# A hybrid gated-attention and Hyena block on one core: the order of high and low products, the opening, the copies out of PSUM and the two layer norms are changed

## The chip, the cores and the metric

The kernel runs on one core of one Trainium2 chip. The metric is device time in microseconds (us) of one execution. Before the change it is 1891.8 us, the median of three runs (1891.52 to 1891.81).

## The reference, cut to what matters

The input is `x`, 256 tokens of 2048 channels, float32. One block is computed:

- One projection `x @ w_in` gives q, k (1024 channels each), v, r (2048 each), two gate vectors of rank 16, `u` (3 x 2048) and `g` (2 x 2048).
- Branch 1 is bidirectional gated linear attention over four heads, with an RMS norm, a SiLU gate from r and an output projection (2048 x 2048).
- Branch 2 is an order-2 Hyena operator: a short convolution splits `u` in v, x1, x2; each of two long convolutions is done by Fourier transforms, with filters that a small sine network makes; then comes an output projection.
- The branches are merged by sigmoid gates and go through `w_out` (2048 x 2048). `z = ALPHA*x + mix`, then a layer norm: `(z - mean) * rsqrt(var + eps) * g + b`.
- An MLP of 2048 -> 8192 -> 2048 with squared ReLU, `z = ALPHA*h + mlp`, and a second layer norm give the output.

Each weight is used once for 256 tokens, and all is float32 in and out.

## The kernel before, in words

**Two-part numbers.** A float32 number is written as a high part (rounded to the type `float32r`, which TensorE multiplies in one pass) and a low part, the remainder. `split_hi_lo` (L80) makes both: ScalarE (ACT in the profile) casts the high part (L81), VectorE (DVE) subtracts to get the low part (L82). A product of two such numbers needs three terms: high*high, high*low, low*high.

**Weights.** All weights lie in `wblk`, in blocks of 128 x 2048 float32 (1 MB), in the order of use. `fetch` (L89) loads a block on SyncE's queue into a `raw` tile (three buffers) and splits it in two halves of 1024 columns (tags `whi` and `wlo`, three half buffers each). Blocks 0 and 1 are loaded in halves, and the transposed input `xT` is loaded in four pieces of 512 KB between the halves of block 0 (`load_x`, L210).

**Two kinds of product.** `channel_pair` (L133) makes outputs with channels on the partitions: two blocks, each one output tile of 128 channels x 256 tokens. For each of 16 k-tiles it issues a high weight product (L143) whose moving operand is the activation's high and low part side by side, 512 columns, and then a low weight product (L144) with the high part alone, 256 columns. Then ACT copies the second half of the PSUM tile (L146), DVE adds it to the first (L147), and `pump` runs side work that has come due (gates, attention scores, filters, transforms, all with times in units of blocks). `token_products` (L151) makes outputs with tokens on the partitions: the activation is the stationary operand, and three products of 512 columns follow each other (L162 to L164) for each token half. `column_products` (L778) does the same in two column halves of 256 (L790 to L792).

**Order.** The program is written in the order opening, gate vectors (`pa`, L367), q, k, r, v with attention, g1, the Hyena stages `u`, g2, `ho`, `w_out`, first norm, then ff1 and ff2 in four quarters, second norm. A scheduler then orders each engine's instructions by a time model; `tc.high_priority()` moves what is under it ahead of other ready work. Each engine runs its own list strictly in order.

**Opening** (L209 to L221): three warm-up products on a zero tile, then the loads above. The constants' loads (`filt_consts`, L237) are issued from ACT's queue.

**Inverse transform** (`hy_inv`, L650): six products of 256 columns for each of two token halves, for 16 pairs of channel group and order.

**First norm** (L813 to L834), per token half `tb`: last products, `add_mix` (L797) with statistics, `norm_scale` (L760), then six column chunks: ACT applies scale and shift (L774), DVE multiplies by the gain row (L775) and adds the bias row (L776). GpSimd (POOL) does the last two for the chunk 1536:2048. `turn` (L822) transposes a chunk on TensorE (L826) and splits it into `hT`. ff1's first output tile takes the first token half before the second (`by_tile`).

**Second norm** (L877 to L886): per token half, `column_products` of the last 512 columns, `add_ff` (L850), `norm_scale`, the same chunks, and a store of each chunk on SyncE's queue (L886).

Of the kernel before, what the change touches and what calls it, by code (L numbers as in the profile page):

```python
# [9 lines left out]
F32 = mybir.dt.float32  # L10
# [30 lines left out]
def block_kernel(  # L41
# [47 lines left out]
    def fetch(between=lambda n, h: None):  # L89
# [5 lines left out]
        if n > 1:  # L95
            nc.sync.dma_start(raw, wblk[n])
        parts = []
        for h in range(2):
            if n <= 1:
                hs = slice(h * D // 2, (h + 1) * D // 2)  # L100
                nc.sync.dma_start(raw[:, hs], wblk[n][:, hs])
                between(n, h)
            hi = wp.tile([P, D // 2], F32R, tag="whi", bufs=3, name=f"whi{n}_{h}")
            lo = wp.tile([P, D // 2], F32R, tag="wlo", bufs=3, name=f"wlo{n}_{h}")
            split_hi_lo(hi, lo, raw[:, h * 1024:(h + 1) * 1024])
            parts.append((hi, lo))
        queue.append(parts)

# [24 lines left out]
    def channel_pair(act, name, dst=None, scale=1.0, by_tile=False):  # L133
        if dst is None:
            dst = base.tile([P, 2, L], F32, tag="sum", name=f"{name}_s")
        for c in range(2):
            ps = psum_main(f"{name}_{c}").rearrange("p (a b) -> p a b", a=2)
            parts = next_block()
            for ts in ((slice(0, P), slice(P, L)) if by_tile and c == 0 else (slice(0, L),)):
                for kt in range(KT):  # L140
                    hi, lo = parts[kt // 8]
                    js = slice(kt % 8 * P, (kt % 8 + 1) * P)
                    MM(ps[:, :, ts], hi[:, js], act[:, kt, :, ts], start=(kt == 0), stop=False)  # L143
                    MM(ps[:, 0, ts], lo[:, js], act[:, kt, 0, ts], start=False, stop=(kt == KT - 1))  # L144
            low = base.tile([P, L], F32, tag="low", name=f"{name}_l{c}")
            nc.scalar.activation(low, ps[:, 1], AF.Copy, scale=scale)  # L146
            nc.vector.scalar_tensor_tensor(dst[:, c], ps[:, 0], scale, low, op0=ALU.mult, op1=ALU.add)  # L147
            pump()
        return dst
# [58 lines left out]

    with tc.tile_pool(name="xp", bufs=1) as xp:  # L209
        def load_x(n, h):  # L210
            for g in (2 * h, 2 * h + 1):
                xr = xp.tile([P, 4, L], F32, tag=f"xr{g}", name=f"xr{g}")
                nc.sync.dma_start(xr, xt[:, 4 * g:4 * g + 4, :])
                split_hi_lo(xT[:, 4 * g:4 * g + 4, 0], xT[:, 4 * g:4 * g + 4, 1], xr)

        wu = xp.tile([P, 512], F32, tag="wu", name="wu")
        nc.vector.memset(wu, 0.0)
        pw = psum_side("warm")
        for _ in range(3):
            MM(pw, wu[:, 0:P], wu, start=True, stop=True)  # L220
        fetch(load_x)  # L221
# [15 lines left out]
    def filt_consts():  # L237
        raw = fp.tile([P, 4, P], F32, tag="w4", name="dftraw")
        nc.scalar.dma_start(raw, dft_in)
        split_hi_lo(dfth, dftl, raw)  # L240
        mw = fp.tile([P, 3, P], F32, tag="mlpw", name="mlpw")
        nc.scalar.dma_start(mw, mlp_w)
        mc = fp.tile([P, 4], F32, tag="mlpc", name="mlpc")
        nc.scalar.dma_start(mc, mlp_c)
        et = fp.tile([P, L], F32, tag="emb", name="emb_sb")
        nc.scalar.dma_start(et, emb)
        nc.scalar.dma_start(ba_sb, ba)
        nc.scalar.dma_start(conv_sb, convp)
        nc.scalar.dma_start(mask_sb, mask_in)
        nc.scalar.dma_start(sgn_sb, sgn_in)  # L250
        nc.scalar.dma_start(ident, ident_in)
        fst["mw"], fst["mc"], fst["g"] = mw, mc, et
# [113 lines left out]

    pa = psum_main("pa").rearrange("p (a b) -> p a b", a=2)  # L367
    fetch()
    parts = next_block()
    for kt in range(KT):  # L370
        hi, lo = parts[kt // 8]
        js = slice(kt % 8 * P, (kt % 8 + 1) * P)
        MM(pa, hi[:, js], xT[:, kt], start=(kt == 0), stop=False)
        MM(pa[:, 0], lo[:, js], xT[:, kt, 0], start=False, stop=(kt == KT - 1))
# [7 lines left out]
    k_sb = qp.tile([P, 8, L], F32, tag="k", name="k_sb")  # L382
    for dst, nm, sc in ((q_sb, "q", 1.0 / 16.0), (k_sb, "k", 1.0)):
        for c2 in range(4):
            channel_pair(xT, f"{nm}{c2}", dst[:, 2 * c2:2 * c2 + 2, :], sc)
# [162 lines left out]
    for h in range(HEADS):  # L548
        later(0, gla_gates(h))
        later(3, gla_scores(h))  # L550
        vh = gp.tile([P, NT, 512], F32R, tag="vh", name=f"vh{h}")
        vl = gp.tile([P, NT, 512], F32R, tag="vl", name=f"vl{h}")
        pss = token_group(xT, f"v{h}")
        for tb in range(NT):
            split_hi_lo(vh[:, tb], vl[:, tb], pss[tb])
        v_sb[h] = (vh, vl)
        later(1, gla_out(h))
# [92 lines left out]
    def hy_inv(c, o):  # L650
        def run():
            yh, yl = cst.pop(("Y", c, o))
            py = psum_side(f"yp{c}{o}")
            for tb in range(NT):
# [114 lines left out]
    CHUNKS = ((0, 256), (256, 256), (1536, 512), (512, 512), (1024, 256), (1280, 256))  # L769

    def norm_chunk(z, rows, tb, at, n, rs, nb):
        zc = z[:, tb, at:at + n]
        eng = nc.gpsimd if at == 1536 else nc.vector
        nc.scalar.activation(zc, zc, AF.Identity, scale=rs, bias=nb)  # L774
        eng.tensor_tensor(zc, zc, rows[:, 0, at:at + n], op=ALU.mult)  # L775
        eng.tensor_tensor(zc, zc, rows[:, 1, at:at + n], op=ALU.add)  # L776
# [36 lines left out]
    for tb in range(NT):  # L813
# [16 lines left out]
        for at, n in CHUNKS:  # L830
            norm_chunk(z1, rows1, tb, at, n, rs, nb)
            if at < 1536:
                turn(at, n)
        turn(1536, 512)  # L834
# [4 lines left out]
    def ff1(qi):  # L839
        f = act_tile(ep, "f", f"f{qi}") if qi % 2 == 0 else act_tile(base, "xT", f"f{qi}")  # L840
        for c2 in range(8):
            r = channel_pair(hT, f"f{qi}_{c2}", by_tile=(qi == 0 and c2 == 0))
# [7 lines left out]
    def add_ff(ps, tb, at, n, qi):  # L850
# [26 lines left out]
    pss = [[psum_main(f"w2_33_{tb}{ch}") for ch in range(2)] for tb in range(NT)]  # L877
    for tb in range(NT):
        column_products(pss, fts[3], parts, [tb], 0)
        with tc.high_priority():  # L880
            for ch in range(2):
                add_ff(pss[tb][ch][:, 0:256], tb, 1536 + ch * 256, 256, 3)
            rs, nb = norm_scale(st2, tb, "2")
        for at, n in CHUNKS:
            norm_chunk(z1, rows2, tb, at, n, rs, nb)
            nc.sync.dma_start(out[tb * P:(tb + 1) * P, at:at + n], z1[:, tb, at:at + n])  # L886
# [127 lines left out]
```

## Time and profile before

| | us |
|---|---|
| median of three runs | 1891.8 |
| the profiled execution | 1891.83 |
| its span in the profile | 1890.0 |
| TensorE (PE) busy | 1860.4 (98%) |
| TensorE weight loads (PEld) busy | 1599.7 (85%) |
| DVE busy | 1313.6 (70%) |
| ACT busy | 949.5 (50%) |
| POOL busy | 38.3 (2%) |
| mean granted TensorE clock | 0.994 |
| traffic with HBM | 198 GB/s |

The profile is one execution. A matmul's recorded duration is longer than the step from its start to the next one's start, because matmuls overlap in the array: L143 shows 394 ns and L144 279 ns, and the two together start every 0.35 us. So TensorE's cost is read from starts, in the timeline, and not from durations. "[3.89 <-DVE xT L82]" behind a row says that the engine was idle for 3.89 us before it, until that DVE instruction ended.

### The profile page before, as it was taken

How to read it: one execution, taken by the hardware profiler on the slowest of the kernel's cores; microseconds unless marked ns; L12 is line 12 of the kernel's file. 1: busy time of each engine (PE TensorE's matmuls, PEld its weight loads, DVE VectorE, ACT ScalarE, POOL GpSimd, SP SyncE). 2: the span in 40 equal slices, each digit the busy share in tenths (PEclk: the TensorE clock that was granted, in tenths of full speed). 3: DMA queues.
4: the chain of work that ended last, by engine and by line, in shares of the span. 5: the costliest groups of instructions: out<-in, count | busy, mean ns of one | idle time of the engine just before them, and what ended most of it. 6: DMA issues, size and time to landing. Idle time of an engine off the chain costs nothing.

```text
span 1890.0 us, 25333 instructions
## 1 busy us (share of the span) xinstructions
PE 1860.4 (98%) x10060; PEld 1599.7 (85%) x10060; DVE 1313.6 (70%) x1702; ACT 949.5 (50%) x1286; POOL 38.3 (2%) x60
## 2 busy tenths in 40 slices
PE   8999999999999999999999998999999999999996
PEld 7887888888888888888888888888888888888886
DVE  6787968875789888888556567666555555555556
ACT  5555556674555555555544444444434443444343
POOL 0000000000000000000000001000000000000001
PEclk9999999999999999999999999999999999999998
DMA  7667764445555555565655764555555555545552
GB/s 289 231 225 251 265 228 161 140 142 204 195 195 199 199 194 189 197 223 191 212 197 183 285 216 153 188 193 186 196 186 198 180 199 187 192 180 199 191 189 110
DMA packets 60583, 375.09 MB, mean 198 GB/s; under 512 B 7216, under 2 KB 10928, under 8 KB 20912
## 3 DMA queue, kind: packets, MB, share of 16 engines
q1 hardware_dynamic: 46512, 324.03, 47.4%
q0 software_dynamic: 5888, 29.36, 4.2%
q10 hardware_dynamic: 8064, 20.07, 3.0%
q8 instruction: 79, 1.29, 0.3%
q14 instruction: 40, 0.33, 0.0%
HBM read 356.66 MB, written 16.78 MB: 198 GB/s over the span
## 4 chain that ended last, share of the span: by engine, by line
PE 93%; DVE 4%; ACT 1%; DMA 1%; issue 1%; ACTq 0%; DVEq 0%; SPq 0%
PE f L143 13%; PE f L144 6%; PE g L143 6%; PE w L163 6%; PE w L164 6%; PE w L162 6%; PE go L143 3%; PE ux L143 3%; PE uz L143 3%; PE uv L143 3%; PE g L144 3%; PE ho L143 3%; PE ho L144 2%; PE uv L144 2%; PE ux L144 2%; PE go L144 2%
## 5 line engine op out<-in xcount | busy, mean ns | idle before, releaser
L82 DVE TENSOR_TENSOR wlo<-raw,whi 128x1024 fp32r<-128x1024 f32 x596 | 728.3, 1223 | 488.2 <-ACT whi L81 487.3
L81 ACT CAST whi<-raw 128x1024 fp32r<-128x1024 f32 x596 | 627.0, 1053 | 772.6 <-PE w L164 186.8
L143 PE MATMUL f<-hT,whi 128*128 128x512 f32 (+1 forms) x1040 | 361.7, 394 | 0.0
L144 PE MATMUL f<-hT,wlo 128*128 128x256 f32 (+1 forms) x1040 | 290.0, 279 | 0.0
L143 PEld LDWEIGHTS f<-hT,whi 128*128 128x128 f32 x1040 | 195.6, 188 | 44.3
L144 PEld LDWEIGHTS f<-hT,wlo 128*128 128x128 f32 x1040 | 197.1, 190 | 0.1
L163 PE MATMUL w<-wlo,f 128*128 128x512 f32 x480 | 186.8, 389 | 0.0
L164 PE MATMUL w<-whi,f 128*128 128x512 f32 x480 | 186.8, 389 | 0.0
L143 PE MATMUL g<-xT,whi 128*128 128x512 f32 x512 | 178.6, 393 | 0.0
L162 PE MATMUL w<-whi,f 128*128 128x512 f32 x480 | 168.0, 389 | 0.0
L144 PE MATMUL g<-xT,wlo 128*128 128x256 f32 x512 | 143.5, 281 | 0.0
L143 PEld LDWEIGHTS g<-xT,whi 128*128 128x128 f32 x512 | 95.7, 187 | 21.1
L162 PEld LDWEIGHTS w<-whi,f 128*128 128x128 f32 x480 | 90.0, 188 | 18.8
L164 PEld LDWEIGHTS w<-whi,f 128*128 128x128 f32 x480 | 90.1, 188 | 18.7
L163 PEld LDWEIGHTS w<-wlo,f 128*128 128x128 f32 x480 | 90.1, 188 | 18.5
L144 PEld LDWEIGHTS g<-xT,wlo 128*128 128x128 f32 x512 | 96.7, 189 | 0.5 <-DVE wlo L82 0.2
L143 PE MATMUL uz<-xT,whi 128*128 128x512 f32 x256 | 91.9, 398 | 0.0
L143 PE MATMUL ux<-xT,whi 128*128 128x512 f32 x256 | 91.7, 398 | 0.0
L143 PE MATMUL go<-yg,whi 128*128 128x512 f32 x256 | 91.1, 397 | 0.0
L143 PE MATMUL uv<-xT,whi 128*128 128x512 f32 x256 | 90.5, 395 | 0.0
L143 PE MATMUL ho<-yh,whi 128*128 128x512 f32 x256 | 88.8, 391 | 0.0
L144 PE MATMUL ux<-xT,wlo 128*128 128x256 f32 x256 | 72.0, 281 | 0.0
(329 smaller groups left out, 3336.7 us busy)
## 6 DMA issues: line engine op xcount, KB each, us to landing
raw<-wblk SPq DMA_DIRECT2D x303, 1024.0 KB, 4.8
Td<-T POOLq DMA_DIRECT2D x16, 768.0 KB, 4.1
Tl<-Td POOLq DMA_DIRECT2D x16, 768.0 KB, 4.5
w<-w4s ACTq DMA_DIRECT2D x16, 512.0 KB, 4.6
zr<-ln_rows ACTq DMA_DIRECT2D x4, 1024.0 KB, 10.9
raw<-wblk SPq DMA_DIRECT2D x4, 512.0 KB, 6.7
xr<-xt SPq DMA_DIRECT2D x4, 512.0 KB, 6.5
dec<-decay_in ACTq DMA_DIRECT2D x8, 256.0 KB, 3.1
```

The source lines that it names most:

```text
L81: nc.scalar.copy(hi, src)
L82: nc.vector.tensor_tensor(lo, src, hi.bitcast(F32), op=ALU.subtract)
L143: MM(ps[:, :, ts], hi[:, js], act[:, kt, :, ts], start=(kt == 0), stop=False)
L144: MM(ps[:, 0, ts], lo[:, js], act[:, kt, 0, ts], start=False, stop=(kt == KT - 1))
L162: MM(pss[tb], sh, wh, start=(kt == 0), stop=False)
L163: MM(pss[tb], sh, wl, start=False, stop=False)
L164: MM(pss[tb], sl, wh, start=False, stop=(kt == KT - 1))
```

## The change

1. **Grouped products.** `channel_pair` issues, for each half of a block, eight high products and then eight low products.
2. **Opening by quarters.** Three blocks (`pa`, and the two of q's first pair) are opened together in three PSUM tiles. Weights and input are loaded in quarters (the first one, for block 0 and the input, in eighths), all issued first. Splits and products follow quarter by quarter.
3. **Constants** are loaded from POOL's queue and not from ACT's.
4. **Copies out of PSUM** of a channel block, and the split of v, stand under `tc.high_priority()`.
5. **`hy_inv`** makes six products of 512 columns, over both token halves.
6. **First norm**: five chunks, none of them on POOL; ff1's first two tiles take three of their four half blocks for the first token half, then for the second.
7. **Second norm**: the gain row is multiplied in when the columns are complete (`add_ff`). Token half 0 gets all 512 columns by `token_products`, and its norm is two DVE instructions per 512 columns (`affine`). For token half 1 TensorE makes `shift*gain + bias` in PSUM from plain float32 products (`ident` x bias row, `dg` x gain row, where `dg` is the identity times the shift), and DVE needs one instruction per chunk.

```diff
+    def channel_products(ps, act, half, kts, ts=FULL, opens=True):
+        hi, lo = half
+        at = [(kt, slice(kt % 8 * P, (kt % 8 + 1) * P)) for kt in kts]
+        for kt, js in at:
+            MM(ps[:, :, ts], hi[:, js], act[:, kt, :, ts], start=(kt == 0 and opens), stop=False)
+        for kt, js in at:
+            MM(ps[:, 0, ts], lo[:, js], act[:, kt, 0, ts], start=False, stop=(kt == KT - 1))
+
+    def channel_sum(dst, ps, name, scale=1.0):
+        low = base.tile([P, L], F32, tag="low", name=name)
+        with tc.high_priority():
+            nc.scalar.activation(low, ps[:, 1], AF.Copy, scale=scale)
+            nc.vector.scalar_tensor_tensor(dst, ps[:, 0], scale, low, op0=ALU.mult, op1=ALU.add)
 ...
+            for h in range(2):
+                channel_products(ps, act, parts[h], range(8 * h, 8 * h + 8))
+            channel_sum(dst[:, c], ps, f"{name}_l{c}", scale)
+            pump()
 ...
+    def channel_pair_by_tokens(act, name):
+        ps = [channel_psum(f"{name}_{c}") for c in range(2)]
+        blocks = [next_block() for _ in range(2)]
+        for ts in (slice(0, P), slice(P, L)):
+            for c, h in ((0, 0), (0, 1), (1, 0)):
+                channel_products(ps[c], act, blocks[c][h], range(8 * h, 8 * h + 8), ts,
+                                 opens=(c == 0 or ts.start == 0))
+        channel_products(ps[1], act, blocks[1][1], range(8, KT))
 ...
-        fetch(load_x)
+        for g in range(4):
+            n = 2 if g == 0 else 1
+            for i in range(n):
+                load_w(0, g, i, n)
+                load_x(g, i, n)
+            for b in range(1, OPENING):
+                load_w(b, g, 0, 1)
+        for g in range(4):
+            pieces = 2 if g == 0 else 1
+            for b in range(OPENING):
 ...
+                for i in range(n):
+                    split_hi_lo(hi[:, at:at + w], lo[:, at:at + w], raws[b][:, cs])
+                    if b == 0:
+                        split_hi_lo(xT[:, ks, 0], xT[:, ks, 1], xr[g][:, step * i:step * (i + 1)])
+                channel_products(open_ps[b], xT, halves_of[b], range(4 * g, 4 * g + 4))
 ...
-        nc.scalar.dma_start(raw, dft_in)
+        nc.gpsimd.dma_start(raw, dft_in)
 ...
-            for tb in range(NT):
-                dst = py[:, tb * CW:(tb + 1) * CW]
-                mm3(dst, dfth[:, 2], dftl[:, 2], yh[:, tb, 0], yl[:, tb, 0], True, False)
-                mm3(dst, dfth[:, 3], dftl[:, 3], yh[:, tb, 1], yl[:, tb, 1], False, True)
+            mm3(py3, dfth[:, 2], dftl[:, 2], yh[:, :, 0], yl[:, :, 0], True, False)
+            mm3(py3, dfth[:, 3], dftl[:, 3], yh[:, :, 1], yl[:, :, 1], False, True)
 ...
-    CHUNKS = ((0, 256), (256, 256), (1536, 512), (512, 512), (1024, 256), (1280, 256))
+    CHUNKS = ((0, 256), (256, 256), (512, 512), (1024, 512), (1536, 512))
 ...
-        eng = nc.gpsimd if at == 1536 else nc.vector
+        nc.vector.tensor_tensor(zc, zc, rows[:, 0, at:at + n], op=ALU.mult)
+        nc.vector.tensor_tensor(zc, zc, rows[:, 1, at:at + n], op=ALU.add)
 ...
+            nc.vector.tensor_tensor(zc, zc, rows2[:, 0, at:at + n], op=ALU.mult)   # add_ff, last quarter
 ...
+    def affine(tb, at, n, rs, nb):
+        nc.vector.scalar_tensor_tensor(t, rows2[:, 0, at:at + n], nb, rows2[:, 1, at:at + n], op0=ALU.mult, op1=ALU.add)
+        nc.vector.scalar_tensor_tensor(zc, zc, rs, t, op0=ALU.mult, op1=ALU.add)
 ...
+    token_products([ps], fts[3], parts, [0], 0)
+    add_ff(ps, 0, 1536, 512, 3)
+    rs, nb = norm_scale(st2, 0, "2")
+    for at in range(0, D, 512):
+        affine(0, at, 512, rs, nb)
+        store(0, at, 512)
+    column_products([None, pss], fts[3], parts, [1], 0)
+    for at, n in BIASED:      # (256, 512), (768, 512), (1280, 512), (1792, 256)
+        po[at] = psum_side(f"lo{at}")[:, 0:n]
+        tc.keep_in_program_order(MM(po[at], ident, rows2[:, 1, at:at + n], start=True, stop=False))
+    for ch in range(2):
+        add_ff(pss[ch][:, 0:256], 1, 1536 + ch * 256, 256, 3)
+    rs, nb = norm_scale(st2, 1, "2")
+    nc.vector.tensor_scalar(dg, ident, nb, None, op0=ALU.mult)
+    affine(1, 0, 256, rs, nb)
+    for at, n in BIASED:
+        MM(po[at], dg, rows2[:, 0, at:at + n], start=False, stop=True)
+        nc.vector.scalar_tensor_tensor(zc, zc, rs, po[at], op0=ALU.mult, op1=ALU.add)
+        store(1, at, n)
```

More of the change, by code (lines that the diff above doesn't have):

```diff
@@ L87, in block_kernel, with fetch @@
     stop_at = [W_OUT_END - 3]
-    def fetch(between=lambda n, h: None):
+    def fetch():
         n = fetched[0]
@@ L107, in fetch, with weight_half @@
         queue.append(parts)
+    def weight_half(n, h):
+        return (wp.tile([P, D // 2], F32R, tag="whi", bufs=3, name=f"whi{n}_{h}"),
+                wp.tile([P, D // 2], F32R, tag="wlo", bufs=3, name=f"wlo{n}_{h}"))
     side = []
@@ L136, in channel_pair @@
         for c in range(2):
-            ps = psum_main(f"{name}_{c}").rearrange("p (a b) -> p a b", a=2)
+            ps = channel_psum(f"{name}_{c}")
             parts = next_block()
[L139 to L147, printed above, removed]
+            for h in range(2):
+                channel_products(ps, act, parts[h], range(8 * h, 8 * h + 8))
+            channel_sum(dst[:, c], ps, f"{name}_l{c}", scale)
+            pump()
+        return dst
+    def channel_pair_by_tokens(act, name):
+        dst = base.tile([P, 2, L], F32, tag="sum", name=f"{name}_s")
+        ps = [channel_psum(f"{name}_{c}") for c in range(2)]
[5 more added lines that the diff above has]
+        channel_products(ps[1], act, blocks[1][1], range(8, KT))
+        for c in range(2):
+            channel_sum(dst[:, c], ps[c], f"{name}_l{c}")
             pump()
@@ L364, in block_kernel @@
         later(n + 2, filt_freq(c, o))
[L367 to L374, printed above, removed]
+    pa = open_ps[0]
     nc.scalar.copy(a_low, pa[:, 1])
@@ L382, in block_kernel @@
     k_sb = qp.tile([P, 8, L], F32, tag="k", name="k_sb")
+    for c in range(2):
+        channel_sum(q_sb[:, c], open_ps[1 + c], f"q0_l{c}", 1.0 / 16.0)
+        pump()
+    for _ in range(2):
+        fetch()
     for dst, nm, sc in ((q_sb, "q", 1.0 / 16.0), (k_sb, "k", 1.0)):
-        for c2 in range(4):
+        for c2 in range(1 if nm == "q" else 0, 4):
             channel_pair(xT, f"{nm}{c2}", dst[:, 2 * c2:2 * c2 + 2, :], sc)
@@ L553, in block_kernel @@
         pss = token_group(xT, f"v{h}")
-        for tb in range(NT):
-            split_hi_lo(vh[:, tb], vl[:, tb], pss[tb])
+        with tc.high_priority():
+            for tb in range(NT):
+                split_hi_lo(vh[:, tb], vl[:, tb], pss[tb])
         v_sb[h] = (vh, vl)
```

86 lines of the change are left out of this document (47 added, 39 removed).

## The prediction

> **What bounds the kernel now.** I read the page first, then busy time by stage, then the timeline of TensorE (PE) where it is not busy.
>
> ```profile
> PE 1860.4 (98%) x10060; PEld 1599.7 (85%) x10060; DVE 1313.6 (70%) x1702; ACT 949.5 (50%) x1286; POOL 38.3 (2%) x60
> ...
> PE 93%; DVE 4%; ACT 1%; DMA 1%; issue 1%; ACTq 0%; DVEq 0%; SPq 0%
> ```
>
> PE is busy 98% of the span and is 93% of the chain that ended last. So time goes only if PE's products get cheaper or its holes close. By stage (columns: length, then busy time of PE, PEld, DVE, ACT, POOL with counts, granted clock, DMA share, GB/s):
>
> ```profile
> 430.00:900.00 470.00, 470.00 (x2750) 412.46 (x2749) 395.52 (x475) 254.29 (x359) 15.23 (x28) 1.00 0.55 198
> ...
> 1128.00:1180.00 52.00, 46.41 (x342) 43.70 (x341) 39.63 (x72) 25.73 (x42) 5.71 (x4) 0.93 0.46 174
> ...
> 1846.00:1890.00 44.00, 29.60 (x220) 28.19 (x219) 26.76 (x53) 13.99 (x22) 6.32 (x4) 0.88 0.25 91
> ```
>
> In the middle PE never stops; holes are in the opening, around the first norm and behind the last product. Durations come from this execution: span 1890.0, its own time 1891.83, which is the median (1891.8). So I subtract from 1891.8.
>
> **1. Grouped products: -7.8.** Weight loads of the high products (L143), counted in two stretches of 80 us that hold nothing else (PE's second figure is the loads):
>
> ```profile
> 1230.00:1310.00 80.00, 80.00 (x232) 43.14 (x231) 1.00 0.54 196
> 1435.00:1515.00 80.00, 80.00 (x227) 42.48 (x227) 1.00 0.53 190
> ```
>
> 80/231 = 0.346 us for one high and one low product, 80/227 = 0.352: the same pair runs at two paces. Two streams of one size have one pace each: ff2's 512-column products start every 0.227 us (1547.48, 1547.71, 1547.94 in the timeline), the last 256-column ones every 0.120 (1856.00, 1856.12, 1856.24). 0.227 + 0.120 = 0.347 is the faster pace, so the slower one pays for the change of size from high to low (0.236 from a high start to the low one, where the fast pace has 0.230). Summed over the starts of the some 2,900 pairs that nothing interrupts, the excess over 0.347 is 8.9 us, 3.4 of it between 1400 and 1700, the rest mostly in q to `go`. Grouping keeps one change in eight: 8.9 x 7/8 = 7.8. Ends: 0 (the pace hangs on something else) and 8.9. Nothing shorter than 0.347 is to be had, as both streams show. What is late next? In 430 to 1100 the low half of a weight block is split at least 1.2 us, mostly 3.4, before its first product; a low product's half now gets 8 x 0.227 = 1.8 us more. The cover is thin only in 100-200 and 250-400, where the lead falls to 0.1.
>
> **2. `hy_inv` at full width: -1.25.** 16 calls lose 12 starts of 0.120 and get 6 of 0.227: 16 x (1.44 - 1.36) = 1.25. Ends 0.5 and 1.5. It lies in 500 to 900, all PE.
>
> **3. Opening: -5.0.**
>
> ```profile
> 3.36 3.02 PE L220 MATMUL warm<-wu 128*128 128x512 f32 x4
> 10.27 0.79 PE L373 MATMUL pa<-xT,whi 128*128 128x512 f32 x1 [3.89 <-DVE xT L82]
> ```
> ```profile
> 9.00:16.00 7.00, 5.73 (x18) 0.51 1.02 393
> ```
>
> PE idles until 10.27; then (second fence: PE's busy time, granted clock, DMA share, GB/s) the clock is halved until 15.9, so that pairs start every 0.64 us. The third block would end at 24.19 + 16 x 0.35 = 29.8 (a side product aside). The changed opening needs 5.24 MB for three blocks. Before has moved 1.2 MB by 7, 2.1 by 9, 3.2 by 12, 4.7 by 16 and 5.2 by 17 us. Taking these times, 0.7 us to landing, ACT casts of 0.6 (512 columns) and 1.05 (1024) and DVE differences of 0.69 and 1.23, the first products follow the warm-up at 6.4, wait once for the input's second eighth (0.8), and quarter 2 starts at 12.1; each quarter is 12 x 0.347 = 4.2 us of PE, so 16.4, 20.6, end 24.8. The fourth block's buffer is free at 18.3, its 1 MB lands at 22.8, cast by 23.9: in time. 29.8 - 24.8 = 5.0. Ends: 1 (the small pieces land as slowly as now, 6.7 us for 512 KB) and 6.5. The constants' loads on POOL's queue are hidden: `dftraw` can go at about 19, is cast behind the fourth block's first half at 24, and the transforms need it 50 us later; POOL's stores of 768 KB land in 4.1 us. If it came later than 25, ACT's next casts stand behind it, 1 us for 1 us.
>
> Here a rule speaks against the change. The Trainium skill (SBUF — State Buffer, on the engine and DMA doors) says that loads issued from POOL wait for descriptors while DVE runs an operation in its two-port mode. No row of before shows a load on POOL in the opening. If `dftraw`, whose issue falls among DVE's splits, waited for four of them at 1.2 us, it would land some 5 us later, and the sum would be 4 worse, which is the far end of the opening's range.
>
> **4. First norm: -2.5.**
>
> ```profile
> 1149.91 1.52 DVE L775 TENSOR_TENSOR zr<-zr 128x256 f32<-128x256 f32 x1
> ```
> ```profile
> 1162.52 0.99 PE L826 MATMUL ht<-ident,zr 128*128 128x128 f32 x4 [1.48 <-DVE zr L776]
> 1166.54 1.51 PE L826 MATMUL ht<-ident,zr 128*128 128x128 f32 x6 [3.03 <-DVE zr L776]
> ```
>
> That DVE product takes 1.52 us instead of 0.43 because POOL works on its chunk from 1149.86 to 1152.58; its neighbour L776 takes 1.51 likewise, and the same happens at 1163.03. Steps from start to start without POOL are 0.34 (256 columns) and 0.61 (512). Laying out DVE's list with these: token half 0 is done as early as now, half 1's shift comes at 1159.4 (now 1160.46), its columns up to 1536 at 1164.4, the last at 1165.7. PE has 24 half-width pairs of 0.23 for half 0 (5.5 us, now 3.7): busy to 1161.8, idle to 1164.9. Left then are 24 x 0.23 + 8 x 0.347 + 0.4 of transposes = 8.7, end 1173.6; now the two tiles end at 1178.6. At full clock that gains 5.0. But in before the clock was halved here (0.66 on average from 1160 to 1170) after idle spells of 1.5 and 3.0, so I expect it again, until about 1169.6: 4.7 us of work at half pace cost 2.3. I take 2.5; ends 1 and 5. The page TensorE: Matmul & The Clock Gate of the Trainium skill (Parts 1 and 4) says that a window of 3.4 us without activity halves the clock, and that transposes do not count as activity; by it the drop comes, and the sum is the one with 2.5.
>
> **5. Second norm: -2.1.**
>
> ```profile
> 1875.64 0.42 DVE L855 TENSOR_TENSOR zr<-zr,w 128x256 f32<-128x256 f32 x1 [1.69 <-PE w L792]
> ```
> ```profile
> 1880.88 2.76 DVE L775 TENSOR_TENSOR zr<-zr 128x512 f32<-128x512 f32 x2 [0.32 <-ACT zr L774]
> ...
> 1884.50 0.74 DVE L776 TENSOR_TENSOR zr<-zr 128x256 f32<-128x256 f32 x2
> ```
>
> Now: last addition 1875.64, shift known 1878.32, last DVE instruction 1885.24, end 1890.0 (store and landing, 4.75, which stays). After: half 0 costs 48 x 0.227 in place of 96 x 0.120, so PE ends 0.6 earlier, last addition at 1875.2 (DVE is still in `affine` of half 0: 8 x 0.61 from 1869). An `affine` instruction of 0.61 and the gain product of 0.34 stand ahead of the aggregate: shift at 1878.6, `dg` 0.2 later. Then TensorE needs 3.5 products of 512 plain float32 columns. The filter network's 256-column float32 products are two records that start 0.32 apart; for 512 I take 2 x 0.53 = 1.06 (ends 0.85, twice the warm-up's cold 0.85 record at full clock, and 1.7 at half clock): 1878.8 + 3.7 + 0.5 for the last DVE instruction and its wait = 1883.1. That gains 2.1; ends -0.3 (half clock) and 2.8. The bias products (3.7 us) lie beside the statistics and keep PE working until 1878.6.
>
> **6. Copies out of PSUM first: 0.** Each channel block has an ACT copy of 0.38 and a DVE sum of 0.42. Moved ahead, they push the next split back by as much, covered by the lead in 1. In q to attention (47 to 430, DVE busy 82%) PE waited 5.2 us in all, in single waits of 0.4 to 1.4 on `wlo`, `T` and `y`. These may go or double: -3 to +4.
>
> Sum: 7.8 + 1.25 + 5.0 + 2.5 + 2.1 = 18.65; 1891.8 - 18.65 = **1873.2**.
>
> **Rivals.**
> - *Grouping does nothing* (the slow pace belongs to the stage and not to the order): 1873.2 + 7.8 = 1881.0. For: the pace differs between equal stages (1230 and 1435). Against: ff2's stream beside it, at 1547, keeps 0.227. Chance 0.13.
> - *The clock holds at the first norm*, since half 0 now has 1.8 us more work: 1871. Against: the idle time is still 3 us. 0.15.
> - *The opening is held by transfers* or by the constants on POOL: gain 0 to 2, 1877. For: landing takes 6.5 us there. 0.10.
> - *The dense stages wait more*: four more waits of about 1 us in 47-430, 1877. 0.10. Or fewer waits and the better ends: 1867. 0.08.
> - *Slower*: the copies stand in ACT's and DVE's lists and wait for a block's last product, and the split behind them comes too late. Place: channel blocks with a lead under 0.8 us. There are some 90 between 47 and 900; were the lead gone in all of them at 0.4 us each, +36, so 1909; it decides from about 47 such blocks on (18.65/0.4). The lead of 1.2 to 3.4 speaks against it. 0.06.
>
> The forecast as summed gets 0.38. Cases within 1866 to 1882 hold over 0.8, so that is the range; the ends of parts 3 to 6 alone reach some 7 either way. A difference under 0.2% (3.8 us) can't be told from none here. Faster 0.92, same 0.02 (the dense stages' case with the worse ends of the others), slower 0.06.
>
> **What would show it.** Grouping: weight loads of the high products at 0.227, of the low ones at 0.120, in all stages. Opening: first real product at 6.4, third block done near 25. First norm: no DVE product of 256 columns above 0.45; two tiles done 5 us after half 1's transposes at full clock, 7 at half. Tail: 12.7 us from the last addition to the end (now 14.4), float32 products at 1.06. Wrong if PE shows holes between 430 and 1100, or pairs above 0.35.

## The result, and the profile after

The changed kernel takes 1883.31 us (median of five runs, 1880.54 to 1886.28) beside 1891.8 (five runs, 1891.52 to 1893.25): ratio 0.9951, 95% interval 0.9938 to 0.9963. It is faster, by 8.5 us and not by 18.6, and lies outside the range of the prediction. The profiled execution took 1880.54, the fastest of the five and 11.3 less than the profiled one before; the comparisons below are between these two. The two slowest of the five show a mean granted clock of 0.996 where the other three show 0.998 or 0.999, and 0.003 of 1880 us is 5.6 us, so by this estimate most of that spread goes with the lower clock.

First the page of the changed kernel: busy time, and the chain that ended last.

```profile
PE 1861.1 (99%) x9948; PEld 1597.5 (85%) x9948; DVE 1313.3 (70%) x1711; ACT 948.8 (51%) x1278; POOL 30.8 (2%) x61
...
PE 96%; DVE 2%; ACT 1%; DMA 0%; issue 0%; SPq 0%; DVEq 0%; ACTq 0%
```

PE has more of the chain (96%, was 93%), and its busy time has not fallen (1861.1, was 1860.4): 6.4 us of it are the new float32 products at the end (3.17 and 3.27), and the other products have not become as cheap as forecast. Busy time by stage (length, PE, PEld, DVE, ACT, POOL, granted clock, DMA share, GB/s; the last two stretches are moved with the stage):

```profile
430.00:900.00 470.00, 470.00 (x2671) 410.99 (x2671) 393.90 (x474) 257.96 (x360) 15.02 (x28) 1.00 0.54 200
1125.00:1177.00 52.00, 49.91 (x380) 47.45 (x379) 42.52 (x76) 27.18 (x42) 0.00 (x0) 1.00 0.52 198
1835.00:1878.60 43.60, 38.79 (x205) 31.50 (x203) 31.28 (x55) 9.67 (x13) 0.00 (x0) 0.99 0.31 120
```

The first norm has few holes left and a full clock (49.9 of 52, was 46.4 at 0.93), and so has the end (38.8 of 43.6, was 29.6 of 44 at 0.88).

Where the 11.3 us come from, by first products in the timeline of PE. "Waits" are steps over 60 ns longer than the stream's own, "pace" the rest above 0.227 or 0.120 us a start; what remains is products moved, added or saved.

| stretch | before | after | difference | of it waits, pace |
|---|---|---|---|---|
| first product to r | 127.6 | 124.9 | -2.7 | -2.6, -0.4 |
| r to v | 130.7 | 126.3 | -4.4 | -1.5, 0; 2.9 of products moved behind v |
| v to `uv` | 212.8 | 219.9 | **+7.1** | **+4.7**, -0.4; 2.7 of products moved in |
| `uv` to `ho` | 504.0 | 501.6 | -2.4 | -0.4, -0.7 |
| `ho`, w_out | 177.3 | 177.8 | +0.5 | 0, +0.6 |
| first norm, ff1's first quarters | 191.1 | 187.8 | -3.3 | -5.5, +1.1 |
| from ff2's first to the last main product | 530.3 | 527.5 | -2.8 | 0, -2.2 |
| last main product to end | 14.6 | 11.5 | -3.2 | |

Two things stand out. Pace has gained about 2 us in all. And g's first product is 8.6 us early (358.8, was 367.4), but `uv`'s first is at 472.6 in both. Not all of the 4.7 us lost there is idle time: right behind the hole shown below, the granted clock was 0.50 from 382.6 to 386.0, and 2.85 us of products ran in that window, which cost some 1.4 us (an estimate: half of 2.85).

### The profile page after: what moved, and what is told of

Same layout as the page of the kernel before. It is cut to its first block, busy times and chain, and to the rows that moved or that the text cites. A ratio compares the mean times of both kernels' runs of the same rounds, so it can differ in the third digit from the quotient of the medians.

```text
span 1878.7 us, 25104 instructions
## 1 busy us (share of the span) xinstructions
PE 1861.1 (99%) x9948; PEld 1597.5 (85%) x9948; DVE 1313.3 (70%) x1711; ACT 948.8 (51%) x1278; POOL 30.8 (2%) x61
## 4 chain that ended last, share of the span: by engine, by line
PE 96%; DVE 2%; ACT 1%; DMA 0%; issue 0%; SPq 0%; DVEq 0%; ACTq 0%
PE f L140 12%; PE f L142 6%; PE g L140 6%; PE w L188 6%; PE w L187 6%; PE w L189 6%; PE uv L140 3%; PE uz L140 3%; PE go L140 3%; PE ux L140 3%; PE ho L140 3%; PE g L142 3%; PE ho L142 2%; PE uv L142 2%; PE go L142 2%; PE ux L142 2%
## 5 line engine op out<-in xcount | busy, mean ns | idle before, releaser
L82 DVE TENSOR_TENSOR wlo<-raw,whi 128x1024 fp32r<-128x1024 f32 (+2 forms) x603 | 729.3, 1211 | 471.9 <-ACT whi L81 451.6
L81 ACT CAST whi<-raw 128x1024 fp32r<-128x1024 f32 (+2 forms) x603 | 627.4, 1041 | 770.7 <-PE w L189 188.8
L140 PE MATMUL f<-hT,whi 128*128 128x512 f32 (+1 forms) x1048 | 258.0, 388 | 0.0
L142 PEld LDWEIGHTS f<-hT,wlo 128*128 128x128 f32 x1048 | 142.3, 190 | 9.8
L142 PE MATMUL f<-hT,wlo 128*128 128x256 f32 (+1 forms) x1048 | 145.5, 282 | 0.0
L140 PE MATMUL g<-xT,whi 128*128 128x512 f32 x512 | 130.5, 396 | 3.7 <-DVE vl L82 3.7
L142 PEld LDWEIGHTS g<-xT,wlo 128*128 128x128 f32 x512 | 69.9, 190 | 5.0
L142 PE MATMUL g<-xT,wlo 128*128 128x256 f32 x512 | 71.8, 282 | 0.0
L140 PE MATMUL uz<-xT,whi 128*128 128x512 f32 x256 | 65.6, 394 | 0.0
L140 PEld LDWEIGHTS go<-yg,whi 128*128 128x128 f32 x256 | 46.1, 189 | 8.3
```

What stands on the lines that cost most here:

```text
L81: nc.scalar.copy(hi, src)
L82: nc.vector.tensor_tensor(lo, src, hi.bitcast(F32), op=ALU.subtract)
```

## The experiments

The three whose names begin with b are the kernel before or edits of it, all others edits of the changed kernel. Ratios are to the kernel before on the same chip, with 95% intervals; the changed kernel's is 0.9951.

### Pace: b0_again, e2_interleaved, e3_group16, b1_grouped

In this part, the excess is what all steps from start to start that nothing interrupts take beyond 0.2267 us (512 columns) and 0.120 us (256), added up.

b0_again is the kernel before, with no edit.

> The kernel before, unchanged, for one more trace. In its first trace a pair of alternating high and low products takes either 346.7 or 353.3 ns and keeps to one of them for as long as nothing comes between (346.7 from 919 to 1344 us, 353.4 from 1425 to 1700). If the pace is fixed by the program, the same stretches show the same pace again and the sum over all pairs is again 8.9 us above .2267 and .120; if it is caught by chance at each break, the long stretches change place, and the time can differ by up to 0.0066 x 900 = 6 us for the stretch from 919 to 1344 alone.

One execution: 1892.0. The pace looks fixed by the program, as far as two executions tell: the excess is 8.9 us again, and the same two stretches hold the same number of weight loads as before:

```profile
1230.00:1310.00 80.00, 80.00 (x232) 43.20 (x231) 1.00 0.54 195
1435.00:1515.00 80.00, 80.00 (x227) 42.56 (x227) 1.00 0.52 190
```

e2_interleaved:
```diff
-        for kt, js in at: MM(high)
-        for kt, js in at: MM(low)
+        for kt, js in at: MM(high); MM(low)
```

> The changed kernel with the high and low products of a block alternating again, all else as changed. The forecast's own rule (grouping takes 7/8 of the excess over 0.347 us a pair): the high and low starts together come back to 8.9 us above .2267 and .120 each, and the median rises by about 7.8 us, to 1891. Theory A (a run of eight high products after low ones runs at 233, 236, 228, 233, 231, 227, 226, 227 ns, so that each change of size still costs about 20 ns net, and grouping took 1.6 us in all): the median rises by 1 to 2 us, to 1885, if the order of the side work stays; in the g stage VectorE's list is the changed kernel's, so its wait at 379 stays.

Both expectations missed. Ratio 1.0011 (1.0000 to 1.0022), so 11.3 us slower than the changed kernel. The excess is 16.3 us: alternating products now keep the slow pace, 353.3 ns a pair, nearly everywhere, also where the kernel before ran at 346.7 (1230 to 1310: 227 loads, were 231). So an alternating stream has two paces and keeps one until something comes between; which one it catches hangs on the program around it. The steps tell more: at the fast pace every pair takes 346 or 347 ns, at the slow one the pairs take 361, 349 and 350 ns in turn, over and over. Size changes in every pair of both, so the change itself is not what the slow pace pays for.

e3_group16, in `channel_pair`:
```diff
-            for h in range(2):
-                channel_products(ps, act, parts[h], range(8 * h, 8 * h + 8))
+            for kt in range(KT): MM(high of parts[kt // 8])
+            for kt in range(KT): MM(low of parts[kt // 8])
```

> The changed kernel with all 16 high products of a block ahead of its 16 low ones (groups of 16 instead of 8; the opening and the block by tokens as they are). Theory A (a transient of some five high products behind each change of size): half the changes go, so the summed excess over .2267 and .120 falls from 7.3 us to about 3.8, the ninth to sixteenth high product start 226 to 227 ns apart, and the median falls by 3 to 4 us. Theory B (a high product with a load of its own costs 230 ns in the mean wherever it stands): the excess stays near 7 us, the median within 1 us but for what a moved side product does.

Ratio 0.9918 (0.9901 to 0.9936): by the ratios 6 us faster than the changed kernel, of which the pace explains 3.4; the rest is within the intervals. The excess is 3.9 us (3.8 expected by theory A). Steps behind a change up in size are 233, 236, 228, 232 and 231 ns, then 226.7 for all eleven others; behind a change down mostly 113 or 114, then 119, then 120. The timeline of PE, first of the changed kernel, then of e3_group16 (start, time, columns, count):

```profile
1241.97 2.00 PE L140 MATMUL f<-hT,whi 128*128 128x512 f32 x8
1243.81 1.12 PE L142 MATMUL f<-hT,wlo 128*128 128x256 f32 x8
1244.76 2.00 PE L140 MATMUL f<-hT,whi 128*128 128x512 f32 x8
```
```profile
1243.47 3.82 PE L158 MATMUL f<-hT,whi 128*128 128x512 f32 x16
1247.13 2.08 PE L160 MATMUL f<-hT,wlo 128*128 128x256 f32 x16
1249.04 2.23 PE L158 MATMUL f<-hT,whi 128*128 128x512 f32 x9
```

Start to start, eight pairs take 2.79 us (348.8 ns a pair), sixteen 5.57 (348.1). One change up in size and one back cost about 20 ns together, whatever the length of the group.

b1_grouped: the kernel before with groups of eight, nothing else.

> The kernel before with grouping by eight in its channel pairs and nothing else of the change. The forecast: 7.8 us faster, 1884. Theory A (1.6 us of pace in all): 1 to 3 us faster, 1889 to 1891, and the summed excess over .2267 and .120 falls from 8.9 to about 7.3 us. Rival (moved side work in the attention stage costs something of its own): slower than 1892, with the loss between g's first product (367.4 before) and uv's first (472.6).

Ratio 0.9974 (0.9964 to 0.9984), 4.9 us faster: between the two. In its trace (2.2 us shorter than before's) the excess falls by 1.3, and waits by 1.0: 1.5 are gone in r and some 0.7 elsewhere, and 1.2 more stand at the first norm (the third block of ff1 starts 25.9 us behind the last product of w_out, was 24.7). So the order alone moves single waits by as much as the pace gives.

### The stretch from v to `uv`: e1_v_plain, e5_v3_first, e4_dve_more, e9_softplus, e13_own_v, b2_own_v

This is the hole in the changed kernel, in the timelines of PE, ACT and DVE:

```profile
379.10 0.39 PE L284 MATMUL o<-vh,stl 128*128 128x512 f32 x1
383.18 1.22 PE L140 MATMUL g<-xT,whi 128*128 128x512 f32 x2 [3.69 <-DVE vl L82]
```
```profile
379.85 1.11 ACT L81 CAST vh<-v 128x512 fp32r<-128x512 f32 x2
```
```profile
381.28 1.27 DVE L503 TENSOR_TENSOR_SCAN gb<-scan_sb,gm 128x256 f32<-128x256 f32 x2
382.46 0.67 DVE L82 TENSOR_TENSOR vl<-v,vh 128x512 fp32r<-128x512 f32 x1
```

Right behind it comes the half clock (length, PE's busy time, granted clock, DMA share, GB/s):

```profile
382.62:386.03 3.41, 2.85 (x7) 0.50 0.00 0
```

g waits for a PSUM tile that holds v_3 (the products of the last head's v), and v_3 is split only now, 20 us behind its last product (358.6). Why?

e1_v_plain:
```diff
-        with tc.high_priority():
-            for tb in range(NT): split_hi_lo(vh[:, tb], ...)
+        for tb in range(NT): split_hi_lo(vh[:, tb], ...)
```

> The changed kernel with the split of v's products at ordinary priority again; channel sums stay at high priority. In VectorE's list the two splits of v_3 then stand ahead of the second direction's scan of head 3 (gb31), as in the kernel before; in the changed kernel they stand behind it. Theory A (that queue order is what cost the 8.5 us between the first product of g at 358.8 and the first of uv at 472.6): the stretch from g's first product to uv's first, 113.8 us in the changed kernel and 105.2 before, falls to 106 to 109, the waits of 3.7 and 1.6 us at 375 to 383 and the half clock at 382.6 go, and the median falls by 4 to 8 us, to about 1877. Theory B (the engines have too much to copy there, and a wait only moves): the stretch stays above 112 and the median within 2 us of the changed kernel's 1883.3.

Ratio 0.9928 (0.9912 to 0.9945). Its interval still overlaps the changed kernel's. The order became what was wanted, but the low part of v_3 comes at 382.4 as before, and g's first to `uv`'s first takes 113.8 us as before. From v's first product the stretch takes 217.8: 2.1 gained, and a wait of 3.0 stays. Theory A is mostly wrong.

e5_v3_first:
```diff
-        later(0, gla_gates(h)); later(3, gla_scores(h))
+        if h < 3: later(0, gla_gates(h)); later(3, gla_scores(h))
...
+        if h == 3: later(0, gla_gates(h)); later(2, gla_scores(h))
-        later(1, gla_out(h))
+        later(1 if h < 3 else 3, gla_out(h))
```

> The changed kernel with the gates of the last head given out behind the split of its v products instead of ahead of it (its scores and output as much later), so that VectorE's and ScalarE's lists hold the split of v_3 ahead of both scans of head 3. Theory A (v_3's split queued behind work that it does not need, on engines that run behind TensorE there, is what holds g): the waits of 1.5 and 3.9 us at 375 to 383 go, v's first product to uv's first falls from 219.9 us to 213 to 215, and the median falls by 4 to 7 us, to about 1878. Theory B (VectorE has 118 us of work in the 120 us from 280 to 400 and TensorE must wait for it somewhere): the waits come back at the outputs or transposes of heads 2 and 3 (about 395 to 430), and the stretch stays above 218.

Theory A falls: ratio 0.9984 (0.9973 to 0.9995). v_3's split still comes at 381, with nothing of head 3 ahead of it, and the last head's later gates cost 9 us at its scores, with the clock at 0.50 from 396.4 to 413.4 (timeline of PE):

```profile
403.33 1.94 PE L562 MATMUL s<-qi,kk 128*128 128x64 f32 x8 [8.87 <-DVE kk L523]
```

e4_dve_more:
```diff
-                nc.vector.tensor_tensor(qi, qh, e1, op=ALU.mult)
+                for _ in range(3): nc.vector.tensor_tensor(qi, qh, e1, op=ALU.mult)
```

> The changed kernel with one VectorE operation of the gates (qi, 128x512, .69 us in the trace) done three times instead of once for each head and direction: 8 x 2 x .6 = 9.6 us more of VectorE's work between 290 and 400, the same values. If VectorE is what the stretch from v to uv waits for (theory B), the last split of v comes about 7 us later, 389 instead of 382.5, and uv's first product (472.6) comes 5 to 9 us later. If only the queue place of v_3's split matters and VectorE has room (theory A), uv's first comes under 3 us later.

One execution, 1891.56. v_3's split moves by 10.9 us (393.4), `uv` by 11.1 (483.7): for theory B, it seemed. But the end of head 2's last output product moves by 10.9 us too (390.4, was 379.5).

e9_softplus, in the gates:
```diff
-  ACT: a = |z + b|;  DVE: m = min(z + b, 0);  ACT: a = ln(1 + exp(-a));  DVE: m = m - a
+  ACT: a = exp(-z - b - 10);  a = ln(a + e^-10);  m = a + 10      (signs turned in what follows)
```

> The changed kernel with VectorE relieved in the attention stage: the log of the gate's sigmoid is computed on ScalarE alone, as -(10 + ln(e^-10 + e^(-z-10))), so that two operations of .48 us and one of .68 go from VectorE for each head and direction, 13.1 us in all between 285 and 385; on ScalarE an exp of 512 columns is replaced by a shift of 512. Theory B (VectorE's work is what the stretch from v to uv waits for; 9.6 us more of it made uv 11.1 us later): the stretch falls from 219.9 us to between 210 and 213, its waits from 11.3 to 2 to 4 us, and the median falls by 7 to 10 us, to about 1875. Theory C (the chain of gates, scores and outputs is a chain of latencies over PE, ScalarE and VectorE, and the added operations only lengthened it): each direction's chain gets shorter by about .5 us, and the stretch falls by under 3 us.

Ratio 0.9934 (0.9920 to 0.9948): 3 us, not 7 to 10; the stretch is 217.0, 2.9 less, which is what theory C allowed. The clock is 1.00 all through it, so some 1.4 of the 2.9 us are the window at half clock that it lacks. v_3's cast comes 2.0 us sooner (377.9), its low part 1.1 (381.4). With 13.1 us of work taken from VectorE, that is too little for its amount of work to be the cause. What these traces share is the row ahead of the hole: v_3's cast follows the end of head 2's last output product, `o<-vh,stl`, by 0.1 to 0.8 us in each, from 377 (e9) to 390 (e4). In all other traces with one buffer for v it follows within 1.1 us, except 2.0 in e8_x_on_act and 2.7 in the kernel before. The tiles `vh` and `vl` have one buffer for all heads; v_3 can't be split before head 2's output has read v_2, and that output stands at the end of gates, scores and masks of head 2 (theory D).

e13_own_v:
```diff
-        vh = gp.tile([P, NT, 512], F32R, tag="vh", name=f"vh{h}")
-        vl = gp.tile([P, NT, 512], F32R, tag="vl", name=f"vl{h}")
+        vh = yT[:, 4 * h:4 * h + 2].rearrange("p a b l -> p a (b l)")
+        vl = yT[:, 4 * h + 2:4 * h + 4].rearrange("p a b l -> p a (b l)")
```

> The changed kernel with v's high and low parts of each head kept in the part of yT that the head's own output fills later, instead of in one buffer vh, vl for all heads. Theory D (v_3 can't leave PSUM before head 2's output products have read v_2, and these come at the end of that head's chain of gates and scores): the split of v_3 follows its last product at once (about 362 instead of 382.5), the waits of 1.5 and 3.9 us at 375 to 383 go, the stretch from v's first product to uv's first falls from 219.9 us to 211 to 215, and the median falls by 5 to 8 us, to about 1877. Theory B (VectorE and ScalarE are too busy there, wherever v stands): the wait comes back at scores or outputs and the stretch stays above 218.

Theory D holds. Ratio 0.9915 (0.9901 to 0.9929), 1877.9. v_3 is cast at once, and g follows v without a hole (timelines of PE and ACT):

```profile
359.97 0.39 PE L189 MATMUL v<-whi,xT 128*128 128x512 f32 x1
360.20 1.98 PE L140 MATMUL g<-xT,whi 128*128 128x512 f32 x8
```
```profile
359.72 1.27 ACT L81 CAST yg<-v 128x512 fp32r<-128x512 f32 x2 [0.79 <-PE v L189]
```

v to `uv` takes 214.1 us, 5.8 less; the waits in it fall from 11.3 to 5.2, and no window at half clock is left in it (some 1.4 of the 5.8).

b2_own_v: the same edit in the kernel before.

> The kernel before with v's own memory and nothing of the change. There TensorE had work until v_3 left PSUM at 383 (no wait in the trace at that place; waits of .6, .9 and 1.1 us stand at the ends of heads 0 to 2). Theory D: the gain is at most those waits and the later 1.4 us, 2 to 4 us, less than in the changed kernel, because the single buffer held nothing back there that was ready. If v's own memory brings as much here as in the changed kernel (5 us or more), the loss was not one that the change had run into.

Ratio 1.0003 (0.9994 to 1.0012): no gain. PE's waits in the stretch fall by 0.9 us (3.3 to 2.4 in the timeline), but the pairs from 425 to 485 have fallen into the slow pace (353.3 ns, were 346.7; 170 loads in 60 us, were 173), which eats it up. So the buffer cost at most about 1 us until PE came 8.6 us earlier; the change ran into it.

### Together: e10_both, e14_own_v_group16, e15_own_v_all

e10_both is e3 and e9 together, e14 is e3 and e13, e15 all three.

> The two that promise most, together: groups of 16 high and 16 low products, and the gate's log sigmoid on ScalarE alone. If the two costs are apart (pace of TensorE in all channel blocks; VectorE in the attention stage), their gains add: 3.4 us of pace and what the relief alone brings (7 to 10 by theory B), so a median near 1871. If the faster pace is again swallowed by VectorE between 250 and 385, less than 2 us beyond the relief alone.

0.9943 (0.9931 to 0.9956): worse than either alone. v to `uv` takes 225.1, with 5.0 us of wait for v_3's split. The single buffer is not all of it: two windows at half clock stand in the stretch (6.83 us from 382.2, 3.41 us from 412.9; 7.85 us of products in them, so some 3.9 us lost), where e9 has none.

> The same with groups of 16 high and 16 low products. If the pace of the channel blocks and the single buffer of v are the two costs that the forecast had wrong, their gains add: 3.4 us of pace beside what v's own memory brings (5 to 8 by theory D), so about 1873 to 1875. By theory B no more than the groups alone, 1878.

0.9885 (0.9870 to 0.9899), 1872.1. Against the changed kernel's 0.9951 the two alone give 3.3 and 3.6 thousandths, together 6.6: the costs are apart.

> The same again with the gate's log sigmoid on ScalarE alone, which brought 3 us by itself and nothing with groups of 16. By theory D what is left of the stretch after v has its own memory is TensorE's own work with small waits, so the relief of VectorE adds under 2 us, either way. By theory B it is here that the relief shows: 5 us or more faster than with v's own memory and groups of 16.

0.9880 (0.9863 to 0.9898), 1871.0: the relief adds 1 us, within the intervals. Theory D's expectation holds. This is the shortest of all, 22 us below the kernel before on the same chip (1892.9) and, by the ratios, 13 below the changed one.

### Opening and first norm: e8_x_on_act, e11_pool_back, e12_one_by_tokens

e8_x_on_act: `nc.sync.dma_start(xr...)` becomes `nc.scalar.dma_start(xr...)`.

> The changed kernel with the five loads of x in the opening issued by ScalarE instead of SyncE, whose 18 issues stretch from 0.7 to 13.7 us. If issuing holds the opening back (theory issue): the second quarter of x lands 1 to 2 us sooner than 11.86, the wait of 2.1 us at 12.1 shrinks below 1, and the last opening product starts at 25 instead of 26.8; the time falls by 1 to 2 us. If the transfers themselves do (theory bytes: some 5 MB are under way on 16 engines at once): x lands no sooner, the last opening product stays within 0.5 us of 26.8, and so does the time.

0.9936 (0.9921 to 0.9952); the interval overlaps the changed kernel's. The second quarter of x is cast 1.3 us sooner (10.5, was 11.9), but the first product starts later (7.1, was 6.0; ACT's casts now stand behind its five issues, 3.3 us) and the last opening product starts at 28.5. Neither theory is borne out: where x gains, weights lose. One trace can't settle more, since 13 traces with the loads unchanged have that product anywhere from 26.3 to 29.0.

e11_pool_back: chunk 1536:2048 of the first norm back on GpSimd, the chunks in their old order.

> The changed kernel with the first norm's last 512 columns on GpSimd again, and the chunks in the order of the kernel before; the two blocks by tokens stay. The forecast's reading: with GpSimd at work VectorE's products of 256 columns take 1.5 instead of .45 us, and the last transposes wait for GpSimd's chunk; the third block of ff1 starts 3 to 5 us later after the last product of wo than the changed kernel's 20.2 us (24 before the change), and the time rises by 3 to 5 us. Rival (the two blocks by tokens alone give the gain): under 1.5 us later.

0.9958 (0.9945 to 0.9972), which the time alone can't tell from 0.9951; the trace can. The third block of ff1 starts 24.2 us behind the last product of w_out (20.2 in the changed kernel), 4 later as expected. Some 1.4 of the 4 are a window at half clock (3.41 us from 1166.4) that the changed kernel's trace lacks; against the traces that have one (21.5 to 21.7) it is 2.6 later. The same DVE product in the changed kernel and in e11:

```profile
1148.11 0.42 DVE L827 TENSOR_TENSOR zr<-zr 128x256 f32<-128x256 f32 x1
```
```profile
1148.48 1.52 DVE L828 TENSOR_TENSOR zr<-zr 128x256 f32<-128x256 f32 x1
```

e12_one_by_tokens:
```diff
-  blocks 0 and 1 of ff1: all products of token half 0 that can go, then half 1
+  block 0 by tokens, block 1 at full width
```

> The changed kernel with only the first block of ff1 by tokens, as in the kernel before; the first norm stays off GpSimd. If the second block by tokens is what fills TensorE while the second half's norm runs: TensorE runs dry about 2.7 us sooner (24 products of 256 columns less ahead of the second half), its wait there grows from 2.3 to about 4 to 5 us, and .6 us of products is saved, so the third block starts 1.5 to 2.5 us later. If VectorE being free of GpSimd gives the whole gain: within .7 us of 20.2.

0.9956 (0.9943 to 0.9970), again not to be told from the changed kernel by time. Third block at 22.5, 2.4 later; PE's waits there are 6.4 us (3.1), its products 0.9 less. Here too a window at half clock stands in the trace (3.41 us from 1162.5), and five of twelve traces with the norm unchanged have one as well. Against those, e12 is 0.9 later, between the two expectations. So the part of GpSimd (with the order of the chunks) is shown; that of the second block by tokens is 0.9 us, or 2.4 if the window comes with it, which one trace can't tell.

## Why the prediction was wrong, step by step

- **1. Grouping, 7.8: about 2.** The failed step is "the slower one pays for the change of size" and "grouping keeps one change in eight". It took one pace of the alternating stream for the price of a change; its 0.236 us from a high start to the low one is one of three steps that take turns there (236, 233, 241 ns). Two equal stretches at two paces in one program (231 and 227 loads) said already that the cost hung on something else; the rival "grouping does nothing" (1881) had the right argument. Groups of 8 run at 348.8 ns a pair, between the two paces of alternation. What the runs showed in its place: some 20 ns for each change up and back, also in groups, and an alternating stream that is at either pace. What decides which pace it catches is open.
- **2. `hy_inv`, 1.25:** 1.3 of products less between `uv` and `ho`. Right.
- **3. Opening, 5.0: 2.6** (waits up to r). First product 6.0, forecast 6.4, and one wait of 0.8 us for the second eighth of x, as forecast; but the second quarter of x was cast at 11.9 and not at about 9.8, so that PE started it at 14.2 and not at 12.1:

```profile
5.99 1.60 PE L140 MATMUL open<-xT,whi 128*128 128x512 f32 x2
8.39 0.73 PE L140 MATMUL open<-xT,whi 128*128 128x512 f32 x2 [0.81 <-DVE xT L82]
...
14.22 0.98 PE L140 MATMUL open<-xT,whi 128*128 128x512 f32 x3 [1.85 <-DVE xT L82]
```

  The failed term is the landing time of the small pieces under 18 loads at once; the forecast's low end had it. Over 13 traces with this opening its last product starts between 26.3 and 29.0; the latest three (28.5 to 29.0) have a window of 3.41 us at half clock in it. `dftraw` on POOL's queue went at 21.9, when DVE was through with x, and was cast at 31.8; nothing on PE waited for it. The rule of the Trainium skill (SBUF — State Buffer, SBUF: two separate sides), that a load issued from POOL waits while DVE is in a two-port mode, showed no price here. It isn't refuted either: DVE's rows there are TENSOR_TENSOR splits, and no row says in which mode they ran.
- **4. First norm, 2.5: about 4.4** (waits -5.5, products +1.1). The layout was right (the two tiles end 8.9 us after PE goes on at 1163.25; laid out: 8.7), and the 2.3 taken off for a halved clock were not due: none in this trace. Of 12 traces with this norm seven keep a full clock there (third block 20.1 to 20.2 us behind w_out) and five show one window of 3.41 us at half clock (21.5 to 21.7), so it costs 1.3 to 1.6; the four traces with the old norm show 6.83 us each. The rule of the Trainium skill (TensorE: Matmul & The Clock Gate, Part 1) on a window of 3.4 us fits the windows' length, 3.41 us. But the forecast took the drop as sure, and with the same idle times of 1.4 and 0.6 us on PE it came in five traces and stayed away in seven; why is open.
- **5. Second norm, 2.1: 3.8** (3.2 behind the last main product, and the 0.6 of products ahead of it, as forecast). The list came out as laid out: 7.9 us from the last addition to the end of DVE's last instruction (forecast 7.9). Its float32 products were cheaper than priced: the first two records start 0.53 us apart, all others 0.43, so 512 columns take 0.86 us and not 1.06; that is the low end that the forecast named:

```profile
1867.55 0.42 DVE L905 TENSOR_TENSOR zr<-zr,w 128x256 f32<-128x256 f32 x1 [1.11 <-PE w L844]
...
1871.14 0.29 DVE L956 TENSOR_SCALAR dg<-ident,lnb 128x128 f32<-128x128 f32 x1
...
1872.64 2.85 DVE L962 SCALAR_TENSOR_TENSOR zr<-zr,lrs,lo 128x512 f32<-128x512 f32 x4 [0.30 <-PE lo L960]
```
```profile
1871.48 3.27 PE L960 MATMUL lo<-zr,dg 128*128 128x512 f32 x8 [0.96 <-DVE dg L956]
```

  What was off is "which stays" for the store: 3.2 us from DVE's last instruction to the end, was 4.75; the last five stores are issued over 3.2 us (1872.4 to 1875.6), where the last four had gone within 1.4. From the last addition to the end it is 11.1 us, forecast 12.7.
- **6. Copies first, 0, with "-3 to +4": +3.2** (4.7 lost between v and `uv`, 1.5 gained in r). The rival "dense stages wait more" named the place and not the cause. The step that failed is a silent one, the sum itself: it let PE's gains ahead of v pass through to the end. What the runs showed in its place: v_3 leaves PSUM only when head 2's output has read v_2 (379.5 in the changed kernel), although PE was through with it at 359; memory of its own for each head's v (e13_own_v) takes 5.8 us off. Of the changed lines, v's priority mark may hold a part (without it, e1, the stretch is 2.1 us shorter in one trace); the mark on the channel copies was left out in no run.

The forecast lacked 7.4 us of the profiled difference (18.65 against 11.3): 5.8 of pace, 3.2 of waits, 2.4 of the opening, less 3.6 that the norms gave beyond it and 0.4 in the rest.

## What to carry to other kernels

A gain on the engine that is always busy reaches the end only if each tile that it hands on is free by then: before adding up, look at every single-buffered tile behind the gain for who reads it last, and when. An overhead computed as "slow pace less fast pace" is no price of an operation until an experiment has changed the number of those operations; where one program shows both paces for the same instructions, suspect a state. And undo a part in the final program, not only in the first one: the excess that groups of eight took away was 1.6 us against one and 9.0 against the other.

## What the runs showed of the hardware

- Alternating float32r products of 512 and 256 columns, each with a weight load, run at 346.7 or 353.3 ns a pair and stay there for as long as blocks follow each other (346.7 from 1176 to 1345 us, 353.3 from 1432 to 1522); the slow pace is a cycle of three pairs, 361, 349 and 350 ns. The same program shows the same pace at the same place in two executions.
- In groups, the first five products of 512 columns behind 256-column ones take 233, 236, 228, 232 and 231 ns, then 226.7; the first of 256 behind 512 gains 6 ns and the second 1. Net, about 20 ns for a change up and back.
- A window at half clock costs about half of its length where PE has work: 1.3 to 1.6 us for 3.41 us at the first norm. Two traces of nearly the same kernel can differ by such a window, so a single trace's gain in a stretch is read with its clock beside it.
- A 128x256 float32 product on VectorE took 1.52 us while GpSimd worked on a 128x512 chunk (1.29 us), 0.42 without.
